# An encoder layer on one core: the order of work changed at five places, among them a filler of the attention's steps

## The chip, the core and the metric

The kernel runs on one core of a Trainium2 chip. TensorE (PE in the profile) multiplies matrices; VectorE (DVE), ScalarE (ACT) and GpSimd (POOL) do the rest; SyncE (SP) and also POOL and ACT issue transfers. The time is that of the device, in microseconds, of one launch; lower is better.

## The reference

One layer of a bidirectional encoder, in float32, with 1024 positions and width 1024. All matrix products are done in three parts (a high and a low half of each operand, without low by low), so that float32's precision is kept.

```python
mod = jax.nn.silu(c) @ w_ada + b_ada              # six rows of 1024: shifts, scales, gates
h = rmsnorm(x, norm1_g) * (1.0 + sc1) + sh1
u, v, q, k, va, gate_a, gate_b = jnp.split(h @ w_in, cuts, axis=-1)
a_out = gmlp_branch(u, v, gm_v_g, gm_w_s, gm_b_s) @ w_a
b_out = window_attention_branch(q, k, va, q_norm_g, k_norm_g, attn_sink) @ w_b
merged = jax.nn.sigmoid(gate_a) * a_out + jax.nn.sigmoid(gate_b) * b_out
x = x + gt1 * (merged @ w_o)
h2 = rmsnorm(x, norm2_g) * (1.0 + sc2) + sh2
f_gate, f_up = jnp.split(h2 @ w_ffn_in, 2, axis=-1)
x = x + gt2 * ((jax.nn.silu(f_gate) * f_up) @ w_ffn_out)
```

The attention branch has 8 query heads on 2 key heads. A block of 128 positions looks at itself and its two neighbours (384 keys, 256 at the ends), with a bias that falls with the distance and a sink logit in the softmax. The gated branch mixes positions in chunks of 128 and multiplies by `gelu(u)`.

## The kernel before

The sequence is worked in two halves of 512 positions by `half(0)` and `half(1)`. After them come the remaining gates (`gate_step`, d = 2 to 7), the output projection with `w_o`, and the feed-forward part (FFN). Gates and FFN use a scheme of Strassen's kind with sums of blocks of the inputs and weights, which needs 7 block products instead of 8; `block_sums` and `prep` make those sums.

**Weights.** A weight unit of 128 x 1024 is loaded as `raw` (by `load`, which issues on SP in the order of the program, or by `store`, which issues on POOL) and split: ACT casts the high half `wh`, DVE (or POOL) subtracts for the low half `wl` (`unit`, `begin_split`, `split2`). PE then needs both halves.

**PSUM.** There are four banks by the name `mm` and four by the name `at`. Each name's banks are handed out in turn, so the fifth tile of a name waits until the first is read.

**The order of the instructions** is that of a scheduler (tile framework), which orders each engine by modelled times, except where the program sets it: `in_order[0] = True`, `after(ins, prev)` (the instruction is issued behind `prev` on its engine, with no wait), and, in FFN, `tc.manual_schedule()`, where the order is that of the code.

**Attention.** In each half, `work` holds 8 pairs of a block and a key head, and the loop over `s` is a pipeline. Step `s` issues on PE the scores of pair `s` (`q_step`: four heads, `at<-kbuf,mid`, two matmuls each), the transposes of pair `s-1`'s probabilities (`transposed`: up to three blocks of four, `at<-ident,lb`), fillers, and the values of pair `s-1` (`values`: `at<-pH,vt` and `at<-pL,vt`). A filler is a piece of 6 matmuls of 128x512 of other products of the half (the u projection and two gates, `mm<-wh,h`), which keep PE busy in the meantime; `FA, FB, FC = 2, 1, 4` says how many stand at which place, and `fill(n)` takes the next `n` of one fixed list. On DVE a step has the reductions of the scores (four, `lb<-at,bias,nsink`: the logits with their bias, and the maximum `nmx`), the low halves of the transposed probabilities (`pL<-at,pH`), the normalising (`normalise`: four `lb<-lb,den`), and the addition of the values (`xs<-at,xs`). On ACT it has the high halves (`pH<-at`), the four exponentials (`lb<-lb,nmx`), the copy of one half of the values (`xs<-at`) and casts. In half 0 each step also squares a row of the other half's x (`hs<-hs`). The `at` banks of a step go, in this order, to its four scores, to the three transposes, and to the values; the banks therefore repeat from step to step, the fourth score taking the bank of the values before.

**Projection of half 0.** `for d in range(KT)` computes the projections with `w_ab`; for `d` of 2 and more a bank's result is copied by ACT (`t<-mm`) and stored to `pd`. In the same loop `x_mod(k)` prepares the input of half 1: it starts the load of x row k+2 (`x_load`, two buffers `hs` and two `xs`), modulates row k on DVE, and makes its high half on ACT (`h<-xs,mod`) and its low half on DVE (`x_low`).

**Conditioning rows.** `ada_half_load` loads a row of `w_ada` in two halves, `ada_half` multiplies it by the silu of c on DVE. Both run in half 1's projection (k of 2 and more), between the low halves of the weights.

**FFN.** `STEPS` has seven products per feature block `f`. After each `product(f, i)` the loop calls `prepare`, which makes the next weight sums and halves, and `evict(f, i)`, which empties a bank: for `i` in 0, 2, 3 before `prepare`, else behind it. `EARLY = 6`.

Of the kernel before, what the change touches and what calls it, by code (L numbers as in the profile page):

```python
# [12 lines left out]
ALU = mybir.AluOpType  # L13
# [25 lines left out]
def kernel(  # L39
# [97 lines left out]
    def load(dst, src):  # L137
        tc.keep_in_program_order(nc.sync.dma_start(dst, src))
# [395 lines left out]

    ada_halves = []

    def ada_half_load(tag="hs"):
        if ada_queue:
            col, gain = ada_queue.pop(0)
            t = [stream(tag) for _ in range(2)]  # L540
            for i in range(2):
                load(t[i], w_ada2[col - GT1][:, i * 512 : (i + 1) * 512])
            ada_halves.append((col, gain, t))

    def ada_pair_load():
# [4 lines left out]
            col, gain = ada_queue.pop(0)  # L550
            ada_ahead.append((col, gain, t[:, j, :]))

    def ada_half(more=None):
        if not ada_halves:
            return
        col, gain, t = ada_halves.pop(0)
        part = sm(16, "part")[:, :1]
        for i, acc_col in enumerate((acc_mod[:, col : col + 1], part)):
            V.scalar_tensor_tensor(out=t[i], in0=t[i], scalar=1.0,
                                   in1=silu_c[:, i * 512 : (i + 1) * 512], op0=ALU.mult,  # L560
                                   op1=ALU.mult, accum_out=acc_col)
        added(acc_mod[:, col : col + 1], part)
        ada_end(col, gain)
        if more:
            ada_half_load(more)
# [7 lines left out]
    def added(dst, src):  # L573
        V.tensor_tensor(dst, dst, src, op=ALU.add)
# [41 lines left out]
        return lambda: V.scalar_tensor_tensor(out=l, in0=src, scalar=bias, in1=h.bitcast(F32),  # L616
                                              op0=ALU.add, op1=ALU.subtract)

    def block_sums(k, part, kinds):
        a0, a1, b0, b1 = (chunk[x] for x in ("a0", "a1", "b0", "b1"))  # L620
        col = lambda t, i: t[:, i : i + 1]
        b11 = lambda: block_part("B11", k, a0, kinds[0], col(mod, SH1 + k))
        b21 = lambda: block_part("B21", k, a1, kinds[0], col(mod, SH1 + 4 + k))
        if part == 0:
            if k == 0:
                V.tensor_scalar(nsh, mod[:, SH1 : SH1 + 8], -1.0, None, op0=ALU.mult)
            low0 = None
            if k == 3:
                low0 = b11()
            V.tensor_tensor(b1, b1, b0, op=ALU.subtract)  # L630
            low3 = block_part("T3", k, b1, kinds[1], col(nsh, k))
            if low0:
                low0()
                low0 = b21()
            V.tensor_tensor(b0, b0, a0, op=ALU.subtract)
            low1 = block_part("T1", k, b0, kinds[1])
            low3()
            if low0:
                low0()
            added(b1, a0)  # L640
            low2 = block_part("T2", k, b1, kinds[1])
            low1()
            block_load(k + 1, "b0")
            low2()
            return
        if k < 3:
            low = b11()
            low1 = b21()
            low()
            block_load(k + 1, "a0")  # L650
            low1()
        V.tensor_tensor(a1, b1, a1, op=ALU.subtract)
        low = block_part("T4", k, a1, kinds[2], col(nsh, 4 + k))
        block_load(k + 1, "b1")
        low()
        block_load(k + 1, "a1")
        for x in blk["B22"]:
            A.activation(x[:, k, :], x[:, k, :].bitcast(F32), AF.Copy, scale=-1.0)
# [91 lines left out]
    def half(hf):  # L750
# [152 lines left out]
        for k in range(KT):  # L903
# [75 lines left out]
                    for i in range(4 * k - 24, 4 * k - 20):  # L979
                        halo_product(i)  # L980
            if hf == 1 and k in (2, 3):
                ada_half_load(("hs", "xs")[k % 2])
            elif hf == 1 and k > 3:
                ada_half(("hs", "xs")[k % 2] if k < 6 else None)
            if k % 2 == 1 and k < KT - 1:
                wq = wq_next
        in_order[0] = False
# [96 lines left out]
        if hf == 0:  # L1084
            def x_spread():
                bc = spread(rcol[1], NT)
                next_x["rb"] = ss_tile()[:, :HALF]
                A.copy(next_x["rb"], bc)

            xks = {}  # L1090

            def x_load(k):
                xks[k] = stream(("hs", "xs")[k % 2])
                load(xks[k], xT[k * P : (k + 1) * P, HALF:])

            def x_mod(k):
                if k == 0:
                    t = [hid() for _ in range(4)]
                    h_next.extend((t[::2], t[1::2]))
                if k + 2 < KT:  # L1100
                    x_load(k + 2)
                if k < KT:
                    xk = xks[k]
                    V.scalar_tensor_tensor(out=xk, in0=xk, scalar=mod[:, SC1 + k : SC1 + k + 1],
                                           in1=next_x["rb"], op0=ALU.mult, op1=ALU.mult)
                    store(x1sd[k], xk)
                    A.activation(h_next[0][k // 4][:, k % 4, :], xk, AF.Identity,
                                 bias=mod[:, SH1 + k : SH1 + k + 1])
                if k:
                    x_low(k - 1)  # L1110

            def x_low(k):
                hi, lo = (t[k // 4][:, k % 4, :] for t in h_next)
                V.scalar_tensor_tensor(out=lo, in0=xks.pop(k),
                                       scalar=mod[:, SH1 + k : SH1 + k + 1],
                                       in1=hi.bitcast(F32), op0=ALU.add, op1=ALU.subtract)
# [68 lines left out]
        for s in range(nw):  # L1185
            if s:
                prepare_due()
                sc = q_step(s)
                pts = transposed(st)
                den = exps(*sc, work[s][1])  # L1190
            fill(FA)
            if hf == 0 and 0 < s < 7:
                x_square(s + 1)
            if hf == 0 and s == 7:
                x_rstd()
            if hf == 0 and s == 5:
                load(silu_d, silu_c)
            normalise(sc[0], sc[2], den)
            if s == 0:
                end_unit()  # L1200
            st = sc[0]
            if s == nw - 1:
                for vg in vgs:
                    act[0] = after(A.activation(vg, vg, AF.Gelu_apprx_tanh), act[0])
                for t, vg in enumerate(vgs[:3]):
                    V.tensor_tensor_reduce(
                        out=stream("hs"), in0=vg, in1=vg, op0=ALU.mult, op1=ALU.add,
                        scale=1.0, scalar=0.0, accum_out=vr[:, t : t + 1])
            if s:
                i, kv = work[s - 1]  # L1210
                values(base + i, koff, kv, pts, vts, i, oH, oL)
            if s == nw - 1:
                A.activation(stream("hs"), vgs[3], AF.Square, accum_out=vr[:, 3:])
                for vg in vgs[:2]:
                    V.tensor_tensor(vg, vg, vgain, op=ALU.mult)
                V.tensor_scalar(vr, vr, 1.0 / GW, EPS, op0=ALU.mult, op1=ALU.add)
                G.tensor_tensor(vr, vr, nhalf[:, :NT], op=ALU.pow)
            fill(FB)
        pts = transposed(st)
        fill(FC)  # L1220
        end_unit = begin_unit()
# [50 lines left out]
        early_raw = []  # L1272

        jobs = []
        if hf == 0:
            ada_load()
            x_spread()
            x_load(0)
            x_load(1)
            jobs.extend((k, lambda k=k: x_mod(k)) for k in range(KT))  # L1280
            jobs.append((7, lambda: x_mod(KT)))
        else:
            apool_ctx.close()
            jpools.append(ffn_ctx.enter_context(pool("j", 6, reuse_waits="tile")))
            kinds[:] = (lambda: midt(F32R, 4)), (lambda: jt(F32R, 4)), hid
            blk["B22"] = (hH[1], hL[1])
            for x in ("b0", "a0", "b1", "a1"):
                block_load(0, x)
            jobs.extend((2 * k + p, lambda k=k, p=p: block_sums(k, p, kinds))
                        for k in range(4) for p in range(2) if k + p < 4)  # L1290

        for d in range(KT):
# [5 lines left out]
            if d == KT - 1:  # L1298
                if hf == 0:
                    early.append(unit(None, V, early_raw[0]))  # L1300
                else:
                    for low in gate_prep_b(2):
                        low()
            if hf and d == 5:
                gate_load(2, store)
            if hf and d == 6:
# [3 lines left out]
            for br, t in ((1, (oH, oL)), (0, (gH, gL))):  # L1310
# [12 lines left out]
                    ms.append(sg)  # L1323
                else:
                    c = tmp()
                    A.copy(c, pb)
                    j = 2 * hf + br
                    nc.scalar.dma_start(pd[d][:, j * Q : (j + 1) * Q], c)
            if d < 2:
# [43 lines left out]
    for d in range(2, KT):  # L1373
        last = d == KT - 1
        in_order[0] = True
        if d == 2:
# [1 line left out]
            gate_evict(d, 0)  # L1378
            held_projection()
            low_c = gate_prep_c(d)  # L1380
            block_sums(3, 1, kinds)
            low_c()
            gate_step(d, 1)
            gate_evict(d, 1)
            gate_load(d + 1)
# [473 lines left out]
    with tc.manual_schedule():  # L1859
# [53 lines left out]
        for f, i in steps:  # L1913
# [3 lines left out]
            if copies:  # L1917
                evict(f, i)
            prepare(u + 2, 1)
            if i == 6 or f < EARLY:  # L1920
                prepare(u + 2, 1)
            if not copies:
                evict(f, i)
            if f and f % 2 == 0 and i == (3 if f >= EARLY else 5):
                later.extend(block_sum.pop(f // 2 - 1))
# [215 lines left out]
```

## Time and profile before

| | |
|---|---|
| three runs | 1235.16, 1231.0, 1232.93 us, median 1232.93 |
| the profiled execution | 1231.51 us, span from the first to the last instruction 1229.7 us |
| busy PE / DVE / ACT / POOL | 1218.5 / 907.9 / 582.2 / 180.8 us |
| granted clock of TensorE | 1.000 of full speed |
| attention of half 0, of half 1 | about 78 to 146 us, 262 to 345 us |
| transfers | 235.76 MB, 192 GB/s over the span |

A group's row in the profile gives line, engine, operation, `output<-inputs`, count, busy time, mean; a timeline row begins with start and duration in us and may end with the idle time before it and what ended it. Nearly all rows have the line 77, that of the helper which issues all of them, so the names tell the rows apart. A PE row's duration includes the pipeline; the cost of a matmul is read from the distance of starts.

### The profile page before, as it was taken

Reading aid. Unit: us, or ns where it says so; the run is one execution under the profiler, and the core shown is the slowest. Engines: PE = TensorE matmul, PEld = TensorE weight load, DVE = VectorE, ACT = ScalarE, POOL = GpSimd, SP = SyncE. Lnnn points to the kernel's source line nnn. Section 1 sums busy time; section 2 is a strip of 40 time slices with the busy share of each in tenths; the row PEclk is TensorE's granted clock in tenths of the full one; section 3 lists DMA queues with packets and bytes.
Section 4 is the critical chain, followed back from the end, with each engine's and each line's share of the span. In section 5 each row is a group of like instructions: output and inputs, shape, how many; then the busy total and the mean of one; then the engine's idle time right before and its main releaser. Section 6 shows DMA issues by size and latency. Waiting matters only on the chain.

```text
span 1229.7 us, 15736 instructions
## 1 busy us (share of the span) xinstructions
PE 1218.5 (99%) x5675; PEld 1012.5 (82%) x5675; DVE 907.9 (74%) x1536; ACT 582.2 (47%) x951; POOL 180.8 (15%) x228
## 2 busy tenths in 40 slices
PE   8999999999999999999999999999999999999998
PEld 6888888888887888888887888888888888888887
DVE  9898884587898798977797766776766766666746
ACT  6668854367876333534453333333333334433342
POOL 1124330023342011222100000100000000010001
PEclk9999999999999999999999999999999999999999
DMA  9633168421157466877413445554655459896552
GB/s 364 251 99 116 39 214 293 138 93 52 60 170 246 158 211 237 293 271 260 183 35 121 153 150 193 205 206 142 217 189 199 173 192 379 319 361 224 189 172 102
DMA packets 78672, 235.76 MB, mean 192 GB/s; under 512 B 9474, under 2 KB 9730, under 8 KB 73603
## 3 DMA queue, kind: packets, MB, share of 16 engines
q1 hardware_dynamic: 56162, 141.43, 33.2%
q0 software_dynamic: 18976, 87.04, 19.5%
q10 hardware_dynamic: 3456, 6.29, 1.4%
q8 instruction: 44, 0.72, 0.2%
q14 instruction: 34, 0.27, 0.1%
HBM read 177.06 MB, written 57.67 MB: 191 GB/s over the span
## 4 chain that ended last, share of the span: by engine, by line
PE 79%; ACT 6%; DVE 6%; DMA 4%; issue 3%; POOL 1%; SPq 0%; DVEq 0%; ACTq 0%; POOLq 0%
PE at L77 42%; PE mm L77 37%; DVE mid L77 2%; ACT mid L77 2%; DVE wl L77 1%; ACT lb L77 1%; ACT wh L77 1%; DVE xs L77 1%; ACT t L77 1%; ACT pH L77 1%; DMA xs<-x1sd 1%; DMA raw<-in_w_kv_dram 1%; DMA hs<-in_w_ada_dram 1%; DMA mid<-in_xo_dram 0%; DMA x1sd<-xs 0%
## 5 line engine op out<-in xcount | busy, mean ns | idle before, releaser
L77 ACT CAST wh<-raw 128x1024 fp32r<-128x1024 f32 (+1 forms) x154 | 160.8, 1046 | 138.5 <-PE at L77 40.2
L77 PE MATMUL mm<-mid,wh 128*128 128x512 f32 x696 | 215.0, 390 | 1.4 <-DVE xs L77 0.9
L77 DVE TENSOR_TENSOR wl<-raw,wh 128x1024 fp32r<-128x1024 f32 (+1 forms) x140 | 170.2, 1219 | 62.4 <-ACT wh L77 61.7
L77 PEld LDWEIGHTS mm<-mid,wh 128*128 128x128 f32 x696 | 130.3, 188 | 29.3 <-issue 1.3
L77 PE MATMUL at<-j,wh 128*128 128x512 f32 x464 | 142.8, 389 | 0.0
L77 PE MATMUL mm<-mid,wl 128*128 128x512 f32 x348 | 135.4, 389 | 0.0
L77 PE MATMUL mm<-wh,h 128*128 128x512 f32 x384 | 129.2, 398 | 1.9 <-ACT h L77 1.9
L77 PEld LDWEIGHTS at<-j,wh 128*128 128x128 f32 x464 | 87.1, 188 | 18.1
L77 DVE TENSOR_TENSOR wl<-ws,wh 128x1024 fp32r<-128x1024 f32 (+1 forms) x53 | 59.1, 1114 | 57.1 <-ACT wh L77 57.1
L77 PE MATMUL at<-j,wl 128*128 128x512 f32 x232 | 90.4, 389 | 0.1
L77 PE MATMUL mm<-j,wh 128*128 128x512 f32 x288 | 88.9, 390 | 0.0
L77 PEld LDWEIGHTS mm<-wh,h 128*128 128x128 f32 x384 | 71.2, 188 | 17.1 <-ACT h L77 3.2
L77 PE MATMUL mm<-h,wh 128*128 128x512 f32 x272 | 84.5, 392 | 0.0
L77 PE MATMUL at<-h,wh 128*128 128x512 f32 x272 | 84.1, 390 | 0.0
L77 PEld LDWEIGHTS mm<-mid,wl 128*128 128x128 f32 x348 | 65.3, 188 | 13.8 <-DVE wl L77 0.2
L77 ACT CAST wh<-ws 128x1024 fp32r<-128x1024 f32 (+1 forms) x53 | 50.9, 961 | 53.7 <-DVE ws L77 35.5
L77 PE MATMUL mm<-wl,h 128*128 128x512 f32 x192 | 75.2, 392 | 0.6 <-DVE wl L77 0.6
L77 PEld LDWEIGHTS mm<-j,wh 128*128 128x128 f32 x288 | 53.9, 188 | 11.1
L77 DVE TENSOR_TENSOR ol<-raw,oh 128x1024 fp32r<-128x1024 f32 x30 | 36.6, 1222 | 31.6 <-ACT oh L77 31.5
L77 PEld LDWEIGHTS at<-h,wh 128*128 128x128 f32 x272 | 50.8, 188 | 10.8 <-DVE mid L77 0.3
L77 PEld LDWEIGHTS mm<-h,wh 128*128 128x128 f32 x272 | 50.6, 188 | 10.4
L77 PE MATMUL mm<-j,wl 128*128 128x512 f32 x144 | 56.3, 391 | 0.2 <-DVE wl L77 0.2
(309 smaller groups left out, 2537.0 us busy)
## 6 DMA issues: line engine op xcount, KB each, us to landing
raw<-in_w_gate_dram SPq DMA_DIRECT2D x28, 512.0 KB, 5.1
tA<-hid POOLq DMA_DIRECT2D x11, 1024.0 KB, 4.9
tB<-hid POOLq DMA_DIRECT2D x11, 1024.0 KB, 5.5
wo<-in_w_out_dram POOLq DMA_DIRECT2D x22, 512.0 KB, 6.6
wS<-wo POOLq DMA_DIRECT2D x11, 1024.0 KB, 5.4
raw<-wS SPq DMA_DIRECT2D x44, 256.0 KB, 3.4
raw<-tB SPq DMA_DIRECT2D x44, 256.0 KB, 4.3
raw<-in_w_out_dram SPq DMA_DIRECT2D x33, 256.0 KB, 5.1
```

The source lines that it names most:

```text
L77: ins = f(*args, **kw)
```

## The change

The same instructions are issued, in another order at five places, but for four loads that move from SP to POOL. (The unchanged numbers FA, FB, FC stay.)

```diff
@@ loop of the attention
             if s:
                 prepare_due()
                 sc = q_step(s)
+                fill(FB)
                 pts = transposed(st)
                 den = exps(*sc, work[s][1])
             fill(FA)
...
-            fill(FB)
+            if s == 0:
+                fill(FB)
         pts = transposed(st)
         fill(FC)
@@ conditioning rows
-    def ada_half_load(tag="hs"):
+    def ada_half_load(tag="hs", queue=load):
...
-                load(t[i], w_ada2[col - GT1][:, i * 512 : (i + 1) * 512])
+                queue(t[i], w_ada2[col - GT1][:, i * 512 : (i + 1) * 512])
...
-    def ada_half(more=None):
+    def ada_half(more=None, prev=None):
...
-            V.scalar_tensor_tensor(out=t[i], in0=t[i], scalar=1.0,
+            after(V.scalar_tensor_tensor(out=t[i], in0=t[i], scalar=1.0,
...
-                                   op1=ALU.mult, accum_out=acc_col)
+                                         op1=ALU.mult, accum_out=acc_col), prev)
...
             if hf == 1 and k in (2, 3):
-                ada_half_load(("hs", "xs")[k % 2])
+                ada_half_load(("hs", "xs")[k % 2], store)
             elif hf == 1 and k > 3:
-                ada_half(("hs", "xs")[k % 2] if k < 6 else None)
+                ada_half(("hs", "xs")[k % 2] if k < 6 else None, unit_low[0])
@@ x rows of half 1, in half 0's projection
             def x_mod(k):
                 if k == 0:
...
+                else:
+                    after(A.activation(h_next[0][(k - 1) // 4][:, (k - 1) % 4, :], xks[k - 1],
+                                       AF.Identity, bias=mod[:, SH1 + k - 1 : SH1 + k]),
+                          bank_copy[0] if k < KT - 1 else None)
                 if k + 2 < KT:
                     x_load(k + 2)
...
                     store(x1sd[k], xk)
-                    A.activation(h_next[0][k // 4][:, k % 4, :], xk, AF.Identity,
-                                 bias=mod[:, SH1 + k : SH1 + k + 1])
                 if k:
                     x_low(k - 1)
...
-                    A.copy(c, pb)
+                    bank_copy[0] = A.copy(c, pb)
@@ block sums
-    def block_sums(k, part, kinds):
+    def block_sums(k, part, kinds, cast=None, last_low=None):
...
+            lows = cast() if cast else ()
             added(b1, a0)
             low2 = block_part("T2", k, b1, kinds[1])
+            for low in lows[:1]:
+                low()
             low1()
             block_load(k + 1, "b0")
             low2()
+            for low in lows[1:]:
+                low()
             return
...
         block_load(k + 1, "b1")
+        if last_low:
+            last_low()
         low()
...
-            jobs.extend((2 * k + p, lambda k=k, p=p: block_sums(k, p, kinds))
+            jobs.extend((2 * k + p, lambda k=k, p=p: block_sums(
+                k, p, kinds, (lambda: gate_prep_b(2)) if k == 3 else None))
...
-                else:
-                    for low in gate_prep_b(2):
-                        low()
...
-            block_sums(3, 1, kinds)
-            low_c()
+            block_sums(3, 1, kinds, None, low_c)
@@ FFN
             prepare(u + 2, 1)
+            if not copies and f < EARLY and i < 6:
+                evict(f, i)
             if i == 6 or f < EARLY:
                 prepare(u + 2, 1)
-            if not copies:
+            if not copies and (f >= EARLY or i == 6):
                 evict(f, i)
```

**PE, a step of the attention in half 0, before.** The numbers behind the names tell tiles apart; `at_1280` is the bank of the values, `at_1305` to `at_1320` are those of the next scores, `mm_996` and `mm_997` belong to the filler, `at_1326` is the first bank of the next transposes.

```order
390 L77 MATMUL at_1280<-pH_1248,vt_694 128x512
391 L77 MATMUL at_1280<-pL_1249,vt_694 128x512
392 L77 MATMUL mm_996<-wh_970,h_238 128x512
393 L77 MATMUL mm_996<-wl_971,h_238 128x512
394 L77 MATMUL mm_996<-wh_970,h_240 128x512
395 L77 MATMUL mm_997<-wh_970,h_238 128x512
396 L77 MATMUL mm_997<-wl_971,h_238 128x512
397 L77 MATMUL mm_997<-wh_970,h_240 128x512
398 L77 MATMUL at_1305<-kbuf,mid_617 128x384 x2
399 L77 MATMUL at_1310<-kbuf,mid_617 128x384 x2
400 L77 MATMUL at_1315<-kbuf,mid_617 128x384 x2
401 L77 MATMUL at_1320<-kbuf,mid_617 128x384 x2
```

The same place on PE now; `at_1286` is the bank of the values here, `mm_994` and `mm_995` are the filler's.

```order
396 L77 MATMUL at_1286<-pH_1254,vt_694 128x512
397 L77 MATMUL at_1286<-pL_1255,vt_694 128x512
398 L77 MATMUL at_1305<-kbuf,mid_617 128x384 x2
399 L77 MATMUL at_1310<-kbuf,mid_617 128x384 x2
400 L77 MATMUL at_1315<-kbuf,mid_617 128x384 x2
401 L77 MATMUL at_1320<-kbuf,mid_617 128x384 x2
402 L77 MATMUL mm_994<-wh_1109,h_238 128x512
403 L77 MATMUL mm_994<-wl_1110,h_238 128x512
404 L77 MATMUL mm_994<-wh_1109,h_240 128x512
405 L77 MATMUL mm_995<-wh_1109,h_238 128x512
406 L77 MATMUL mm_995<-wl_1110,h_238 128x512
407 L77 MATMUL mm_995<-wh_1109,h_240 128x512
```

The filler has moved from between values and scores to between the scores and the transposes that follow at row 408 (row 402 before); the scores now come directly behind the values.

**ACT, in half 0's projection, before.** `h_1959` and `h_1961` are the high halves of half 1's input (rows 0 to 3 and 4 to 7), from x rows in `hs` and `xs`; `t` are the bank copies.

```order
215 L77 CAST wh_2060<-raw_2020 128x1024
216 L77 ACTIVATE h_1959<-hs_1963,mod 128x512
217 L77 COPY t_392_2035<-mm_2022 128x512
218 L1328 DMA pd<-t_392_2035 128x512
219 L77 ACTIVATE h_1959<-xs_2008,mod 128x512
220 L77 ACTIVATE h_1961<-hs_2054,mod 128x512
221 L77 COPY t_394_2051<-mm_2038 128x512
```

And now, from the same cast:

```order
214 L77 CAST wh_2059<-raw_2019 128x1024
215 L77 COPY t_392_2034<-mm_2021 128x512
216 L1339 DMA pd<-t_392_2034 128x512
217 L77 CAST wh_2103<-raw_2063 128x1024
218 L77 COPY t_394_2050<-mm_2037 128x512
219 L77 ACTIVATE h_1959<-xs_1927,mod 128x512
```

The bank copies now stand ahead; the high half from `xs_1927` (x row 1), which stood at row 213, ahead of the cast, comes behind two of them, and those of rows 2 and 3 come behind it in turn.

**DVE, the gates' first step behind half 1 and, further on, an FFN step.** `wl_4215` is the low half of a gate weight, `h_3887` that of a block sum; in FFN `xs_6358<-mm_5958` empties a bank and `wl_6380` is a weight's low half.

```order
 L77 TENSOR_TENSOR hs_4096<-xs_4093,hs_4096 128x512
+L77 TENSOR_TENSOR wl_4215<-raw_4049,wh_4214 128x1024
 L77 SCALAR_TENSOR_TENSOR h_3887<-hs_4096,nsh,h_3886 128x512
-L77 TENSOR_TENSOR wl_4215<-raw_4049,wh_4214 128x1024
 L77 TENSOR_TENSOR mid_4197<-mm_4223,xs_4195 128x512
```

```order
 L77 SCALAR_TENSOR_TENSOR ws_5855<-ws_5855,raw_6151 128x512
+L77 TENSOR_TENSOR xs_6358<-mm_5958,xs_6358 128x512
 L77 TENSOR_TENSOR wl_6380<-ws_5855,wh_6379 128x1024
-L77 TENSOR_TENSOR xs_6358<-mm_5958,xs_6358 128x512
 L77 TENSOR_TENSOR xs_6335<-at_6345,xs_6335 128x512
```

In the first, the weight's low half has moved ahead of the block sum's; in the second, the bank's eviction has moved ahead of the weight's low half (the same at three more steps).

More of the change, by code (lines that the diff above doesn't have):

```diff
@@ L558, in ada_half @@
         for i, acc_col in enumerate((acc_mod[:, col : col + 1], part)):
-            V.scalar_tensor_tensor(out=t[i], in0=t[i], scalar=1.0,
-                                   in1=silu_c[:, i * 512 : (i + 1) * 512], op0=ALU.mult,
-                                   op1=ALU.mult, accum_out=acc_col)
+            after(V.scalar_tensor_tensor(out=t[i], in0=t[i], scalar=1.0,
+                                         in1=silu_c[:, i * 512 : (i + 1) * 512], op0=ALU.mult,
+                                         op1=ALU.mult, accum_out=acc_col), prev)
         added(acc_mod[:, col : col + 1], part)
@@ L1088, in x_spread @@
                 A.copy(next_x["rb"], bc)
-            xks = {}
+            xks, bank_copy = {}, [None]
             def x_load(k):
@@ L1274, in half @@
         jobs = []
+        if hf == 1:
+            bank_copy = [None]
         if hf == 0:
```

## The prediction

> **What bounds the kernel now.** I read the page first, then PE's waits, the chain of waits, and the timeline of an attention step and of single stalls. From the page, and from the table of what PE waited for:
>
> ```profile
> PE 1218.5 (99%) x5675; PEld 1012.5 (82%) x5675; DVE 907.9 (74%) x1536; ACT 582.2 (47%) x951; POOL 180.8 (15%) x228
> PEclk9999999999999999999999999999999999999999
> ...
> PE mm L77 <- DVE xs L77: 0.9, 1, 0.9
> PE mm L77 <- DVE wl L77: 0.8, 2, 0.6
> PE mm L77 <- ACT t L77: 0.6, 1, 0.6
> ```
>
> PE is busy for 99% at full clock, and the table holds a few microseconds. So the kernel has little to win: only a wait that PE really makes. It has much to lose: any place where an engine now finishes shortly before PE needs it. The attention steps are such a place. The chain of waits through a step of half 0:
>
> ```profile
> 111.53 1.84 PE at L77 x12
> 114.42 0.59 ACT pH L77
> 115.01 2.40 ACT lb L77 x8
> 117.95 1.41 DVE lb L77 x4
> 119.39 0.71 DVE xs L77
> ```
>
> That is: PE's transposes, ACT's copies of them (pH), the exponentials, DVE's normalising, DVE's addition of the values (xs). A step of half 1, from the timelines of PE, ACT and DVE, shows the same pieces and how much time stands between them:
>
> ```profile
> 289.94 1.57 PE L77 MATMUL at<-ident,lb 128*128 128x128 f32 x12
> 291.27 0.49 PE L77 MATMUL mm<-wh,h 128*128 128x512 f32 x1
> 294.13 0.39 PE L77 MATMUL at<-pH,vt 128*128 128x512 f32 x1
> 295.51 0.39 PE L77 MATMUL mm<-wh,h 128*128 128x512 f32 x1
> 296.90 1.55 PE L77 MATMUL at<-kbuf,mid 128*128 128x384 f32 x8
> 298.29 0.93 PE L77 MATMUL at<-ident,lb 128*128 128x128 f32 x7
> ...
> 290.63 1.57 ACT L77 CAST pH<-at 128x512 fp32r<-128x512 f32 x3
> 292.09 0.62 ACT L77 ACTIVATE lb<-lb,nmx 128x384 f32<-128x384 f32 x1
> 295.77 0.59 ACT L77 COPY xs<-at 64x512 f32<-64x512 f32 x1 [1.08 <-PE at L77]
> ...
> 295.13 1.41 DVE L77 TENSOR_SCALAR lb<-lb,den 128x384 f32<-128x384 f32 x4
> 296.46 0.68 DVE L77 TENSOR_TENSOR xs<-at,xs 64x512 f32<-64x512 f32 x1
> 297.45 0.62 DVE L77 CUSTOM_DVE_ANT_0 lb<-at,bias,nsink 128x384 f32<-128x384 f32 x1 [0.32 <-PE at L77]
> ```
>
> From start to start on PE: transposes 1.33, two fillers (12 matmuls) 2.86, values 1.38, one filler 1.39, scores 1.39, in all 8.35 us, which is the sum of the work. From the start of the transposes, the addition ends 296.46 + 0.68 - 289.94 = 7.20 us later.
>
> **The change: the attention's filler.** The filler is moved by some matmuls, none is added. What matters is who waits for the addition. The `at` pool has four banks; a step takes three for transposes, one for values, four for scores, so the fourth score's bank is the one that held the values, and it comes free when DVE has added them up. Before, that score starts 6.96 + 0.75 x 1.39 = 8.00 us after the transposes, 0.80 after the addition: no wait. Now the values are followed directly by the scores, and the fourth starts at the earliest 1.33 + 2.86 + 1.38 + 1.04 = 6.61 us after the transposes. The addition isn't earlier, since nothing ahead of it moved: pH waits for the transposes, the exponentials for ACT, the normalising for the last exponential, and DVE does the addition behind it. So PE waits 7.20 - 6.61 = 0.59 us, and about 0.06 to wake. The filler stands behind the wait and can't cover it; the fourth score (0.35) and the filler (1.39) then follow, so that the step lasts 7.20 + 0.06 + 0.35 + 1.39 = 9.00 us instead of 8.35. DVE's reductions of the scores and their transposes, which the filler now separates, no longer wait for each other, but in the step above the pieces add up to the step, so that is worth 0.15 us at most.
>
> A loop has six such steps in each half, 6 x 0.65 = 3.9 us. The first transposes come 1.39 later, because the filler of that step now stands ahead of them; at the loop's end it is missing behind the last values, where the transposes of the last step then wait for their normalising, so that only about 0.3 of it comes back in half 0 and none in half 1, whose last steps are narrower. That makes 5.0 and 5.3.
>
> ACT gets one more hindrance. The copies of the finished u products (two pairs) fall elsewhere, since the filler that finishes them moved: one pair stands now ahead of the values' copy in step 4, the other ahead of pH in step 5.
>
> ```profile
> 109.11 0.62 ACT L77 ACTIVATE hs<-hs 128x512 f32<-128x512 f32 x1
> ...
> L77 ACT COPY mid<-mm 128x512 f32<-128x512 f32 x4 | 2.1, 580 | 0.0
> ```
>
> In half 0 the pair (2 x 0.53) and the squares of x (0.62) stand ahead of the values' copy: after the last exponential (four of 0.6 from 292.09 on, and 0.2 for the sink's: 4.75 us behind the transposes) they run to about 6.6, the copy to 7.2, the addition to 8.0 instead of 7.2: +0.8, and +0.1 for the other pair. In half 1 there are no squares, +0.1. Attention in all: 5.9 + 5.4 = 11.3 us. As ends I keep +6, if half of the latency shrinks because ACT is relieved of other work at that place, and +14, if the additions end as late as 7.4 to 7.8 behind the transposes.
>
> **The other places** take away stalls. Their sizes, from the timelines of PE, DVE and ACT:
>
> ```profile
> 194.23 0.39 PE L77 MATMUL mm<-mid,wl 128*128 128x512 f32 x1
> 194.56 0.56 ACT L77 COPY t<-mm 128x512 f32<-128x512 f32 x1
> 195.18 0.74 PE L77 MATMUL mm<-mid,wh 128*128 128x512 f32 x2 [0.56 <-ACT t L77]
> ...
> 216.53 1.22 DVE L77 TENSOR_TENSOR wl<-raw,wh 128x1024 fp32r<-128x1024 f32 x1
> 216.78 0.40 PE L77 MATMUL mm<-wh,h 128*128 128x512 f32 x1
> 217.81 0.50 PE L77 MATMUL mm<-wl,h 128*128 128x512 f32 x1 [0.63 <-DVE wl L77]
> ...
> 392.14 0.61 PE L77 MATMUL mm<-j,wh 128*128 128x512 f32 x2
> 392.95 0.50 PE L77 MATMUL mm<-j,wl 128*128 128x512 f32 x1 [0.20 <-DVE wl L77]
> 398.07 0.61 PE L77 MATMUL at<-j,wh 128*128 128x512 f32 x2
> 398.81 0.50 PE L77 MATMUL at<-j,wl 128*128 128x512 f32 x1
> ...
> 666.36 0.39 PE L77 MATMUL at<-j,wl 128*128 128x512 f32 x1
> 666.77 0.68 DVE L77 TENSOR_TENSOR xs<-mm,xs 128x512 f32<-128x512 f32 x1
> 667.61 0.70 PE L77 MATMUL mm<-mid,wh 128*128 128x512 f32 x2 [0.86 <-DVE xs L77]
> ```
>
> Matmuls of this size follow each other at 0.23 us (1.39 for six, above); what is over that between two starts is a stall, with about 0.1 more behind it.
> - FFN, eviction between the two preparations: 667.61 - 666.36 - 0.23 = 1.02, with the 0.1: -1.1 us. The weight half (wl) that now runs behind the eviction has a step of 2.7 us before its use, so it is hidden; if it were not, its 0.68 us delay would be the price once in each of the four places, less what is left of that step.
> - Weight halves ahead of the block sums' low halves: 392.95 - 392.14 - 0.45 = 0.36 and 398.81 - 398.07 - 0.45 = 0.29, with 0.1 each: -0.87. The low halves now come later by 1.2; their products stand several products behind.
> - x rows modulated one step later, and the ada dots behind the weight half with two pairs of loads on POOL's queue. The stalls are 195.18 - 194.23 - 0.23 = 0.72 (a bank's copy on ACT behind a modulation that waits for its load) and 217.81 - 216.78 - 0.23 = 0.80 (wl behind a dot that waits for its load), 1.9 with what follows. But the low halves of x come later, with them the buffers of the x loads, and SP's queue issues in order:
>
> ```profile
> 188.09 0.33 SPq L138 DMA_DIRECT2D xs<-in_xT_dram  x1
> 191.39 0.33 SPq L138 DMA_DIRECT2D raw<-in_w_q_dram  x1
> ...
> 200.04 1.05 ACT L77 CAST wh<-raw 128x1024 fp32r<-128x1024 f32 x1 [0.45 <-ACT t L77]
> ```
>
> By the new order the last x load waits for the low half of x row 3, about 199.8 instead of 188.09, and the q weight behind it is issued at about 200.2 instead of 191.39. With a landing of some 5 us ACT can't cast it at 200.04 but at 205, and it blocks the bank copies behind it; I count 0.2, 0.6, 0.9 and 0.2 us of new waits in half 1's first products, 1.9 us. Behind the modulation, which now waits for the bank's copy, ACT has only the next cast and copy, and POOL's queue, which gets four loads, has the stores of the x rows, so neither adds to this. I take 0; the ends are -1.9, if nothing is late, and +3, if the k and next q weights behind it are late as well.
>
> **Sum.** 11.3 - 1.1 - 0.9 + 0 = +9.3 us on the profiled execution of 1231.51 (span 1229.7), 1240.8. The median of the three runs, 1232.93, lies 1.4 above that execution; I take a value nearer to the profile, 1241.5.
>
> **Rivals.**
> - The move is a gain (the other side: faster). If the addition ends within 6.6 us of the transposes, the fourth score doesn't wait, the transposes no longer wait for reductions, and 14 steps gain 0.1 to 0.15 us, at most 2; with the stalls gone the time is 1231.5 - 2 - 2 = 1227.5, and 1225.6 with the x stage. The point that decides is that 6.6. For it: pH may start sooner, as ACT's casts of the step before are out of the way by then. Against it: in half 1 pH starts 0.69 behind the transposes as it is, and 0.6 us would have to go. Chance 0.1.
> - Half of the latency goes, because of the same relief, and the x stage gains its 1.9: 6 - 2 - 1.9 = +2.1, 1234, within the noise. Chance 0.12.
> - The q weight's lateness adds its +3: 1244 to 1246. A part of the main case's range.
> - The clock. PE's stalls of 0.80 and 1.02 us stand in slices with PEclk 9, so this trace shows no loss of clock by such stalls; twelve shorter ones are unlikely to. Were the clock to fall by half there, sixteen steps of 8.35 us would last twice as long, 134 us more, 1365. Chance 0.02, outside the range. [...]
>
> [...]
>
> **How the numbers follow.** A measurement of this kernel tells 0.3% (3.7 us) from no change, so the bounds lie at 1229.2 and 1236.6. The main case has 0.76, its own range is 1236 to 1247, and 0.01 of it lies within the noise; the second rival has 0.12, within; the first 0.10, faster; the clock 0.02, slower. Faster 0.10, same 0.13, slower 0.77. The range of 1233 to 1247 leaves out the first rival, the clock and about 0.06 at the ends of the rest.
>
> **What the changed profile would show.** Right: about twelve waits of PE (`at<-kbuf,mid`, the fourth score) on DVE's addition `xs<-at,xs`, 0.5 to 0.9 each; steps of 9.0 us from transposes to transposes; no wait of transposes on reductions; no stalls near 392, 398 and 666 (shifted); new waits at half 1's first products, clock full. Wrong: steps of 8.4 us or less, or an addition that ends within 6.6 us of the transposes. Then the latency I carried over from before is the step that fails.

## The result, and the profile after

The changed kernel takes 1248.52 us (median of five runs, 1246.98 to 1250.44), before 1232.93: ratio 1.0133, interval 1.0119 to 1.0146. It is slower by 15.6 us, where 8.6 were forecast. The profiled execution took 1248.35, span 1246.6. The page and the table of PE's waits of the changed kernel:

```profile
PE 1225.1 (98%) x5675; PEld 1014.5 (81%) x5675; DVE 905.5 (73%) x1536; ACT 582.1 (47%) x951; POOL 183.0 (15%) x232
PEclk9999999989999999999999999999999999999999
...
PE at L77 <- DVE xs L77: 9.2, 12, 1.3
PE mm L77 <- ACT mid L77: 3.5, 1, 3.5
PE mm L77 <- ACT h L77: 1.6, 4, 0.7
...
PE mm L77 <- ACT wh L77: 0.8, 1, 0.8
```

The first wait is the one forecast: twelve times, 9.2 us. The second and the last were not in the forecast, nor was the slice with a clock below 9. Where the 16.9 us of span came in, by the same instructions in both traces:

| | before | after | later by | added here |
|---|---|---|---|---|
| end of half 0's last transposes | 146.39 | 152.46 | 6.1 | 6.1 attention, half 0 |
| half 1's first scores | 262.55 | 274.76 | 12.2 | 6.1 x rows and conditioning rows |
| end of half 1's last transposes | 329.44 | 347.53 | 18.1 | 5.9 attention, half 1 |
| end of the span | 1229.7 | 1246.6 | 16.9 | -1.2 block sums, FFN |

**Attention.** One step of half 1 in the changed kernel, PE's timeline and then DVE's:

```profile
305.10 1.47 PE L77 MATMUL at<-ident,lb 128*128 128x128 f32 x12
306.32 0.48 PE L77 MATMUL mm<-wh,h 128*128 128x512 f32 x1
309.18 0.39 PE L77 MATMUL at<-pH,vt 128*128 128x512 f32 x1
310.56 1.20 PE L77 MATMUL at<-kbuf,mid 128*128 128x384 f32 x6
312.33 0.62 PE L77 MATMUL at<-kbuf,mid 128*128 128x384 f32 x2 [0.56 <-DVE xs L77]
312.79 0.39 PE L77 MATMUL mm<-wh,h 128*128 128x512 f32 x1
314.18 0.49 PE L77 MATMUL at<-ident,lb 128*128 128x128 f32 x3
...
311.60 0.68 DVE L77 TENSOR_TENSOR xs<-at,xs 64x512 f32<-64x512 f32 x1
```

Three scores (six matmuls) run, the fourth waits for the addition, which ends at 312.28, 7.18 us behind the transposes. The step is 314.18 - 305.10 = 9.08 us; from the fourth score to the filler it takes 0.46 (312.79 - 312.33), where four scores followed each other at 0.35 before. The transposes now take 1.22 instead of 1.33: before, one of them started only at 290.86, behind a reduction that ended at 290.79, and now they follow each other at 0.11 without a break; but what PE saves there it waits longer at the fourth score.

**Half 1's projection.** Before, a conditioning row's dot on DVE, the next rows' load and the q and v weights on SP:

```profile
208.51 0.68 DVE L77 SCALAR_TENSOR_TENSOR hs<-hs,silu_c 128x512 f32<-128x512 f32 x1
...
212.16 1.02 SPq L138 DMA_DIRECT2D hs<-in_w_ada_dram  x2
217.78 0.33 SPq L138 DMA_DIRECT2D raw<-in_w_q_dram  x1
225.04 10.49 SPq L138 DMA_DIRECT2D raw<-in_w_v_dram  x4
```

Now, from the timelines of DVE, SP, ACT and PE, in this order:

```profile
230.51 1.23 DVE L77 TENSOR_TENSOR wl<-raw,wh 128x1024 fp32r<-128x1024 f32 x1 [6.41 <-ACT wh L77]
231.66 0.69 DVE L77 SCALAR_TENSOR_TENSOR hs<-hs,silu_c 128x512 f32<-128x512 f32 x1
240.38 0.68 DVE L77 SCALAR_TENSOR_TENSOR xs<-xs,silu_c 128x512 f32<-128x512 f32 x1
...
232.38 0.94 SPq L138 DMA_DIRECT2D hs<-in_w_ada_dram  x2
233.41 0.38 SPq L138 DMA_DIRECT2D raw<-in_w_q_dram  x1
241.10 0.94 SPq L138 DMA_DIRECT2D xs<-in_w_ada_dram  x2
...
238.16 1.05 ACT L77 CAST wh<-raw 128x1024 fp32r<-128x1024 f32 x1 [7.68 <-DMA raw<-in_w_q_dram]
248.06 1.04 ACT L77 CAST wh<-raw 128x1024 fp32r<-128x1024 f32 x1 [8.85 <-DMA raw<-in_w_v_dram]
249.01 1.07 ACT L77 COPY mid<-mm 128x512 f32<-128x512 f32 x2
...
239.26 1.21 PE L77 MATMUL mm<-wh,h 128*128 128x512 f32 x4 [0.81 <-ACT wh L77]
249.64 0.79 PE L77 MATMUL mm<-wh,h 128*128 128x512 f32 x1 [3.50 <-ACT mid L77]
```

Read as a chain. The dot of a conditioning row (`hs<-hs,silu_c`) stands behind a weight's low half at 230.51, which itself waited 6.4 us for its cast. The dot frees the `hs` buffer, and at once, at 232.38, SP issues the next row's load into it. That load had stood at the head of SP's queue (by the waits of SP for 20.2 us); behind it stood the q weight, issued at 233.41; before, it was issued at 217.78, so that beside the 6 us that everything is later here it lost 9.5. Its cast comes at 238.16, and PE waits. With the `xs` buffer the same happens once more: the v weights go out behind the load of 241.10, the cast at 248.06 waits for the first, and ACT's copies of the full banks stand behind that cast. PE has no bank and waits from 246.0 to 249.64, and 0.5 us more for the low half.

And then the clock. Busy time and PEclk by stretch in the changed kernel (after the sums: mean granted clock, share of the DMA engines, GB/s):

```profile
246.00:248.00 2.00, 0.14 (x2) 0.00 (x0) 0.51 (x4) 0.00 (x0) 0.00 (x0) 1.00 0.98 397
249.00:250.00 1.00, 0.36 (x1) 0.29 (x1) 0.87 (x1) 1.00 (x4) 0.00 (x0) 0.53 0.26 107
252.00:255.00 3.00, 3.00 (x9) 2.32 (x8) 2.93 (x8) 2.70 (x11) 1.11 (x1) 0.50 0.68 194
256.00:257.00 1.00, 1.00 (x6) 0.81 (x5) 1.00 (x3) 0.74 (x2) 1.00 (x2) 1.00 0.00 0
```

PE works at half clock (0.50) for some 5.5 us, which costs 2.6 us (13 matmuls at 0.43 instead of 0.23). 1.1 + 4.2 + 2.6 us of new loss, less the 1.7 of the two stalls that are gone (0.72 and 0.80, with 0.1 behind each), makes 6.2; the table has 6.1.

### The profile page after: what moved, and what is told of

The parts are those of the page before. It is cut to its first block, busy times and chain, and to the rows that moved or that the text cites. A ratio compares the mean times of both kernels' runs of the same rounds, so it can differ in the third digit from the quotient of the medians.

```text
span 1246.6 us, 15734 instructions
## 1 busy us (share of the span) xinstructions
PE 1225.1 (98%) x5675; PEld 1014.5 (81%) x5675; DVE 905.5 (73%) x1536; ACT 582.1 (47%) x951; POOL 183.0 (15%) x232
## 4 chain that ended last, share of the span: by engine, by line
PE 88%; DVE 5%; ACT 4%; DMA 2%; issue 1%; SPq 0%; DVEq 0%; ACTq 0%
PE mm L77 46%; PE at L77 42%; ACT lb L77 2%; DVE mid L77 1%; DVE lb L77 1%; ACT pH L77 1%; DMA raw<-in_w_q_dram 1%; DVE xs L77 1%; DVE wl L77 1%; DMA raw<-in_w_v_dram 0%; ACT wh L77 0%; DMA mid<-in_xo_dram 0%; DVE den L77 0%; ACT mid L77 0%; DVE h L77 0%
```

## The experiments

All are compared with the kernel before, run beside them on the same chip. The changed kernel was not run again there, so where a run is set against it the ratios to before are the safer measure.

**Each place alone.** `e1_filler` is before with only the two edits of `fill(FB)`; `e2_ada` has only the edit of the conditioning rows; `e3_xrows` only that of `x_mod`; `e4_sums_ffn` only those of `block_sums` and of FFN. Their diffs are the parts of the change shown above.

> Before, with the filler's move alone. Theory (the fourth score waits for the addition of the values): attention costs 11 to 12.5 us as in the changed kernel, steps of 9.0 to 9.2 us, some twelve waits of the fourth score on the addition; time 1243.5 to 1246. Rival (much of the changed kernel's loss in attention is carried in by late weights from the other edits): under 8 us, 1241 or less.

Measured: 1245.2 us, ratio 1.0099 (1.0082 to 1.0116), +12.6; PE waits on the addition 12 times, 9.3 us. The attention's loss doesn't come from the other edits.

> Before, with the edit of the conditioning rows alone (loads on POOL's queue and the dots behind the weight's low half). Theory A (the dots come late, keep the buffers of the next rows' loads, and SP's queue holds the q and v weights behind those loads): PE stalls of about 1 and 3.7 us in half 1's projection and behind it, and half clock for some 5 us after the longer one; +5 to +8 us, 1238 to 1241. Rival B (the x rows' late low halves make the q weights late, as I had forecast): no such stalls here, -0.8 us, 1232.

Measured: 1238.87 us, 1.0052 (1.0033 to 1.0071), +6.3. Theory A. The same chain stands here without the x rows' edit: the loads at 226.62 and 235.47, the q and v weights behind them, waits of 0.9 and 2.5 us, a half clock of 6.8 us that begins in the longer one.

> Before, with the edit of the x rows alone. Theory A: the stall of 0.7 us at the bank copy goes, at most 0.3 us of new waits at half 1's start, -0.3 to -0.8 us, 1232.3. Rival B: the last x load and the q weight behind it come about 10 us later and cost 2 to 6 us, 1235 to 1239.

Measured: 1231.02 us, 0.9989 (0.9978 to 1.0000). Both stalls, at 194 and at 217, are gone, though nothing was done to the second here; at half 1's start 0.2 us is new. Rival B, my own forecast for this place, falls: in this profile the last x load goes out at 196.83 and the q weight at 197.21, so they are late (188.09 and 191.39 before), but half 1 feels it with 0.2 us and not with 1.9.

> Before, with the edits of the block sums and of the FFN alone. Theory: the stalls near 392, 398 and 666 go (1.9 us with what follows them), a new one of about 0.2 comes near 400: -1.2 to -1.9 us, 1231.3. Rival (the moved work makes other waits): within 0.5 us of before.

Measured: 1229.35 us, 0.9977 (0.9968 to 0.9986), -2.8 by the ratio and -3.3 by the medians, more than expected. The three stalls are gone. In the profiled execution of the changed kernel the same edits are worth 1.2 by the table above, in which other small waits differ too.

**The conditioning rows taken apart.** `e5_ada_pool` has only the loads on POOL's queue, `e6_ada_order` only the order of the dots, `e7_no_order` is the changed kernel with this undone:

```diff
-                ada_half(("hs", "xs")[k % 2] if k < 6 else None, unit_low[0])
+                ada_half(("hs", "xs")[k % 2] if k < 6 else None)
```

> Before, with the four loads of conditioning rows on POOL's queue, the dots where they were. Theory A (it is the order of the dots that costs): no stall near 232 and 240, the q and v weights are issued as early as before or earlier; the wait of a weight's low half behind a dot (0.8 us) may go, since the rows land earlier or don't: 1231.5 to 1233. Rival C (rows loaded by POOL land so late that the dots and what is behind them are late): +3 us or more, 1236.

Measured: 1235.49 us, 1.0028 (1.0014 to 1.0043). Neither clean case: PE waits 2.6 us at the bank copy of 194 (0.7 before) and 1.2 near 206 for a low half that stands behind a dot, whose row POOL loaded late. A part of rival C is true.

> Before, with the dots behind the weight's low half, all loads on SP. Theory A: like both together, the dots come at about 225 and 234 instead of 206 and 216, so that the next rows' loads and the weights behind them on SP come 9 to 10 us late: 1238 to 1241. Rival C: 1232 to 1233.

Measured: 1238.18 us, 1.0047 (1.0034 to 1.0061). The order by itself makes the chain, with loads on SP: they go out at 226.91 and 235.64, PE waits 0.8 and 2.7 us, and the clock is halved for 3.4 us.

> The changed kernel with only the order of the dots undone (four other places and the loads on POOL stay). Theory A: the stalls of 1.0 and 3.7 us and the half clock behind them go, about 6 to 7 us less than the changed kernel: 1241 to 1243. Rival B (the x rows' late low halves, which this leaves in): 1245 or more.

Measured: 1247.76 us, 1.0126 (1.0111 to 1.0142): only 0.8 us less than the changed kernel (1.0133), which is within the noise. Theory A fails, and the time is the one that rival B named. The timelines of DVE, POOL and PE show what took the stall's place:

```profile
215.58 0.75 DVE L77 SCALAR_TENSOR_TENSOR h<-xs,mod,h 128x512 fp32r<-128x512 f32 x1
222.59 0.69 DVE L77 SCALAR_TENSOR_TENSOR xs<-xs,silu_c 128x512 f32<-128x512 f32 x1 [4.69 <-issue]
224.02 1.22 DVE L77 TENSOR_TENSOR wl<-raw,wh 128x1024 fp32r<-128x1024 f32 x1
...
216.63 0.54 POOL L141 DMA_DIRECT2D xs<-in_w_ada_dram  x1 [3.57 <-DVE h L77]
...
225.29 0.50 PE L77 MATMUL mm<-wl,h 128*128 128x512 f32 x1 [2.51 <-DVE wl L77]
```

POOL's load of the row's second half waits until the late low half of an x row (215.58) frees its buffer; the dot waits for the load until 222.59, and the weight's low half (224.02) stands behind the dot. PE loses 2.7 us there, and the clock is halved again, for 3.4 us. So the two edits each make a loss that the other hides: with the order, the dots hold up the loads; without it, the late loads hold up the low half behind the dots.

> The changed kernel without the whole edit of the conditioning rows (neither order nor POOL's loads). Theory (the loads on POOL are what made the x rows' lateness cost in the run without the dots' order: they wait on POOL for the buffers that the late low halves free, and the weight's low half waits behind their dots): no stall over 0.5 us near half 1's start, full clock there, 1241 to 1242.5. Rival (the x rows' edit costs by itself as soon as attention's steps are longer): 1245 or more.

`e10_no_ada` is the changed kernel without either part of the conditioning rows' edit. Measured: 1241.55 us, 1.0083 (1.0064 to 1.0102), less than the changed kernel by 6.2 us by the ratios, 7.0 by the medians; no wait over 0.25 us near half 1's start, clock 1.000. The x rows' edit costs nothing beside the longer attention; the loads on POOL, which wait for the late low halves, were the other half of it.

**The fourth score.** `e8_gap` moves the filler to between the third and the fourth score, and takes it from the steps' end:

```diff
+            if gap and j == QPK - 1:
+                gap()
             ps = at_bank()
...
-                sc = q_step(s)
+                sc = q_step(s, lambda: fill(FB))
```

> Before, with the filler between the third and the fourth score, and not at the step's end. Theory (only the fourth score waits, for the bank of the values): its first matmul now stands 8.0 us behind the transposes, after the addition, so that the twelve waits go and the steps are 8.3 to 8.4 us; the transposes of the probabilities wait a little less for reductions: 1231 to 1233. Rival (the chain through exponentials, normalising and transposes sets the step whatever PE does between): steps of 9 us, 1243.

Measured: 1233.65 us, 1.0013 (1.0003 to 1.0023), just above what was expected. PE's timeline, then DVE's:

```profile
299.92 1.47 PE L77 MATMUL at<-ident,lb 128*128 128x128 f32 x12
305.39 1.20 PE L77 MATMUL at<-kbuf,mid 128*128 128x384 f32 x6
307.80 0.51 PE L77 MATMUL at<-kbuf,mid 128*128 128x384 f32 x2
308.15 0.38 PE L77 MATMUL at<-ident,lb 128*128 128x128 f32 x2
...
306.55 0.69 DVE L77 TENSOR_TENSOR xs<-at,xs 64x512 f32<-64x512 f32 x1
```

The addition ends at 307.24, the fourth score starts at 307.80 without a wait, and the step lasts 8.23 us. The chain through exponentials and normalising is as long as in the changed kernel, 7.3 us (7.18 there); so it is the bank, and what stands behind its wait, that set the 9.08. The whole isn't faster than before, where the fourth score had no wait either. Half 0's last transposes end 1.5 us later than before: 0.5 of it was there before the attention began, and without the filler in front of them they take 2.10 us instead of 1.47.

**Combinations.** `e9_three` has x rows, block sums and FFN; `e11_gap_end` has these, the split scores and one filler at the end of the last step (`if s in (0, nw - 1): fill(FB)`).

> Before, with the x rows, block sums and FFN edits, without the attention's and the conditioning rows' edits. Theory (the three remove stalls and share no queue or buffer that is late): -1.4 and -2.9 add up, 1228 to 1229. Rival (as in the kernel without the dots' order, the x rows' late low halves cost as soon as something else is with them): 1231 or more.

Measured: 1229.34 us, 0.9983 (0.9972 to 0.9993). The two stalls of the projection and those of 392, 398 and 666 are gone together, yet by the ratios it is no faster than block sums and FFN alone; that they add up is not shown. In its profile it is 2.0 us ahead of before at the end of half 1's last transposes (327.40 against 329.44) but only 0.6 at the end of the span. Two waits in the gates, near 404 and 482, are part of what was lost, 1.3 us together; both are for the halves of gate weights that landed late (ACT's casts wait for `raw<-in_w_ga_dram`). Whether the other runs have them is not known.

> As the kernel with three edits, with the filler between the third and fourth score, and one filler more at the end of the last step, so that the last transposes don't wait for their normalising. Theory: steps of 8.2 us in half 1 (8.35 before), no wait at the loop's end: 0.5 to 2 us less than the kernel with three edits, 1227. Rival (ACT's copies ahead of the values' copy make half 0's steps longer by as much): the same as that kernel.

Measured: 1229.94 us, 0.9985 (0.9970 to 0.9999). The steps are 8.2 us, but half 0's last transposes still end 1.2 us later than before, with one filler (1.4 us) more in front of them, and the time is that of `e9_three`. Both are faster than the changed kernel, and than before by nearly 0.2%.

**The clock by itself.** `e12_idle` is before, with four operations more ahead of one addition in FFN:

```diff
+            if f == 2:
+                for _ in range(4):
+                    V.tensor_tensor(keep[f, "c"], keep[f, "c"], keep[f, "c"], op=ALU.max)
             V.tensor_tensor(keep[f, "c"], a, keep[f, "c"], op=ALU.add)
```

> Before, with four operations on DVE (0.68 us each, x = max(x, x)) ahead of the addition that PE waits for in the first FFN step with that wait (near 666). It lengthens PE's stall there from 1.0 to about 3.7 us, far from half 1's start, with nothing else changed. Theory (an idle of about 3 us by itself halves the granted clock for some 5 us): PEclk near 0.5 behind it, +2.7 of wait and +2 to 3 of slow matmuls. Rival (the half clock in half 1 has to do with what else happens there): +2.7 us, clock full.

Measured: 1237.49 us (one run), waits of PE 3.8 us, and this in the stretches:

```profile
667.00:669.00 2.00, 0.06 (x1) 0.00 (x0) 1.93 (x4) 0.00 (x0) 0.00 (x0) 1.00 0.00 0
670.00:671.00 1.00, 0.14 (x1) 0.17 (x2) 0.98 (x2) 0.00 (x0) 0.00 (x0) 0.50 0.00 0
672.00:676.00 4.00, 4.00 (x11) 3.14 (x10) 1.74 (x2) 1.04 (x1) 0.00 (x0) 0.50 0.43 133
677.00:678.00 1.00, 1.00 (x6) 0.80 (x6) 0.65 (x2) 0.00 (x0) 0.00 (x0) 1.00 0.00 0
```

In an idle of 4.0 us, in the middle of FFN, the granted clock fell to 0.50 and stayed there for 6.8 us. In this run the half clock came without anything of half 1's projection.

## Why the prediction was right or wrong

- **Attention, +11.3: right, 12.0 in the profile.** The mechanism was as worked out: the latency 7.18 us (7.20 carried over), twelve waits, steps of 9.08 (9.00). `e8_gap` shows the cause, not only the coincidence. That the sum came so near is in part luck. The steps cost 10.7 us where 8.8 were counted, and the waits were 0.35 to 1.34, not 0.5 to 0.9. The fourth score took 0.46 and not 0.35, some steps have a latency of 7.31, and three steps whose own work had been only 7.6 to 7.9 us lost 0.9 to 1.2 instead of 0.65: a step that is set by the latency is not much shorter for having less work. Against this, the ends of the two loops gave back 1.4 us and not 0.3.
- **Block sums and FFN, -2.0: right in kind.** The three stalls went; `e4_sums_ffn` gives -2.8 by its ratio, the profile of the change -1.2.
- **x rows and conditioning rows, 0 (ends -1.9 and +3): wrong, +6.1.** Of the 7.6 us by which the profile lies above the sum (16.9 against 9.3) this makes 6.1; attention adds 0.7, block sums and FFN 0.8. This is the step that failed, in two ways. The gain of 1.9 was reckoned from what stands ahead of the delayed dots; what waits for the dots was left out. They free the buffers of the next rows' loads, and on SP those loads stand ahead of the q and v weights. I followed such a chain for the x loads, where `e3_xrows` shows that it costs 0.2 us, and not for the dots, where it costs 5 to 6 (`e6_ada_order`). And "POOL's queue ... has the stores of the x rows, so neither adds to this" was wrong: by `e5_ada_pool` the loads there cost 0.3% by themselves (how they bring its wait of 2.6 us is open), and in `e7_no_order` they keep the loss alive. The 1.9 for the stalls is also 0.2 more than their rows give, which changes little.
- **The clock.** I gave it 0.02, in the attention. That it might fall by half there was an assumption, and no run shows it: with twelve waits of up to 1.3 us it stayed at 1.00. It fell where I had seen no stall, to 0.50, and cost 2.6 us of the profiled execution.
- **The other rivals.** That the move is a gain fell with the 7.18 us, that half of the latency goes likewise. That the wait repeated in the steps is one for the bank holds by `e8_gap`: it keeps the latency (7.3 us), gives the bank 0.56 us more than it needs, and the wait is gone.

Open: why x row 7 landed later in `e5_ada_pool` (modulated at 194.80, 193.15 before), and whether the gate weights that were late in the profile of `e9_three` are why it gains no more than `e4_sums_ffn`.

## What to carry to other kernels

When an instruction is moved later, list what it frees, not only what it waits for: a buffer, then the load that waits for the buffer, then everything behind that load in its queue. When work is moved out of the place ahead of a wait, the work no longer covers it; put filler directly ahead of the one instruction that waits, as between the third and the fourth score here, where the waits went and the time was again about that of before. Undoing one of two edits that both hold up the same path shows little (0.8 us here) though each costs several microseconds by itself; try each alone as well.

## What the runs showed of the hardware that was not expected

In five of the profiled executions PE's granted clock fell to 0.50 at a pause; at other pauses it stayed at 1.00. An idle is counted here as the distance of two starts less the cost of the matmul between. The twelve waits of the attention, up to 1.5 us by this measure, and one of 2.6 (`e5_ada_pool`, near 194) left the clock at 1.00. Two of 2.7 (`e2_ada`, near 241, and `e7_no_order`), one of 2.9 (`e6_ada_order`, near 241), and those of 3.7 and 4.0 us (the changed kernel, `e12_idle`) halved it. The half clock lasted 3.4 us in `e6_ada_order` and `e7_no_order` and 6.8 us in the other three, so that an idle of 2.7 us gave both. In the changed kernel and in `e12_idle` the clock fell while PE still idled, 0.6 and 1.0 us before it began again. In `e7_no_order` it fell about 1 us after PE had begun again:

```profile
225.00:226.00 1.00, 0.71 (x3) 0.62 (x4) 0.97 (x4) 0.00 (x0) 0.00 (x0) 1.00 0.00 0
226.00:227.00 1.00, 1.00 (x5) 0.77 (x4) 0.38 (x2) 0.00 (x0) 0.00 (x0) 0.62 0.65 123
227.00:229.00 2.00, 2.00 (x10) 1.81 (x9) 0.00 (x0) 0.00 (x0) 0.00 (x0) 0.50 0.92 339
```

The length of the idle alone does not tell these cases apart: 2.6 us left the clock at 1.00, and 2.7 us came with 3.4 us of half clock in one run and 6.8 us in another. No run moves one idle of a fixed length to other times, so what else counts is not shown, and the 2.6 us that did no harm is no safe length.
